# Sums of a seven-product layer moved to DVE and spread over earlier steps, norm spreads a step later, first residual reread from the input

## The chip, the cores and the metric

One core of a Trainium2 chip runs the whole program. The metric is the device time of one execution in microseconds (us), as the median of several runs. Five engines work from queues of their own, each in order: TensorE (PE) does matmuls, with its weight loads shown apart as PEld; VectorE (DVE), ScalarE (ACT) and GpSimd (POOL) do elementwise work; SyncE (SP) issues the DMAs.

## The reference

Two layers of a diffusion backbone over 512 latent and 256 context tokens of width 1024. Each layer is: a half-step SwiGLU FFN of width 2816, a token mixer, and a second half-step FFN.

```python
x = x + 0.5 * mod[2] * swiglu(modulate(x, mod[0], mod[1]), ffn1_w1, ffn1_w3, ffn1_w2)
...                              # the mixer, with mod[3..5]
x = x + 0.5 * mod[8] * swiglu(modulate(x, mod[6], mod[7]), ffn2_w1, ffn2_w3, ffn2_w2)

def modulate(x, shift, scale):
    return rms_norm(x) * (1 + scale) + shift
def swiglu(h, w1, w3, w2):
    return (jax.nn.silu(h @ w1) * (h @ w3)) @ w2
```

The context rows go through the same weights; in the second layer they stop after the mixer's keys. The nine vectors `mod` (adaLN) come from a 1024 x 9216 map of the conditioning.

## The kernel before, in words

Activations lie transposed: 128 features on the partitions, tokens along the row. `X` holds the residual in four tiles, `xn` the normalized input in eight tiles of 128 features, each as a high and a low half (`fp32r`), so that a product is three matmuls (`mm3`, L343 to L345): high by high, high by low, low by high. The tokens are worked in chunks: CL is all 512 latent ones, CLA and CLB their halves, CC the 256 of the context.

**Weights.** The class `Weights` reads the stream of weights in order. A unit is six blocks of 128 x 128, a set piece is four. `_make` splits one into halves: ACT copies the high half (L234), POOL subtracts (L235); for a set DVE adds some pieces first (L252 to L257). `ahead` is called at fixed places of the product loops and makes the next piece if it is within `ahead_by` units of the one in use. All tiles of 6 KB a row (`xn`, `X`, weights, `xs`, `xq`, hidden pairs, adaLN blocks) share 28 slots.

**The seven-product layers.** Three of the four FFNs (l=0 which=1 and 2, l=1 which=1) go through `ffn`. The first four hidden blocks (ff 0 to 3) are computed plainly: `up2_gen` makes ff 0 and 1 together, 16 steps for a chunk; `up_gen` makes one ff in four steps for a chunk, w1 first, then w3. Each ends in `tail`: ACT's silu into `gst` (L909), and a product with the second bank on DVE (L910). In the first FFN, which has two chunks, ff 0, 1 and the latent part of 2 come first, then ff 0, 1 of the context, then the list `rest`: (2, CC), (3, CL), (3, CC). In the other two, with three chunks, `rest` begins with (2, CL). The other 18 blocks are made pairwise by `seven_gen`: each pair and each of w1, w3 is a 2 x 2 block product in seven products instead of eight (tiles `sv`). Four of the seven read sums of the input blocks, which `Sums` prepares.

**Sums.** For each pair of feature tiles (i, i + 4) one job over two token blocks (the latent part) and one over the third (the context part): two additions of high and low halves into `xq` on POOL (L779), four operations that combine them on DVE (L782 to L785), two copies of the high half into `xs` on ACT (L788) and two differences on DVE (L789). Eight jobs, in two steps each, all placed between the steps of `rest`.

**Between the steps.** `cond` loads the conditioning and keeps its silu in PSUM for DVE; `more` does quarters of the adaLN map on DVE (L421) in the steps of `rest` after the first product, then after each of the seven products, at an even pace set by `calls`; `keep` stores a hidden pair and `save_x` the residual; `late` (the function `lambdas`) is a short chain of DVE and ACT operations with an exponential, once, in the first FFN.

**Norms.** `norm_gen` gives the next product its input in steps: `root` (column sums by PE, DVE, a power on POOL), `diag` (DVE builds `dg`, L529), `spread` (two or four matmuls of `dg` against ones, L543, which PE can do only when `dg` is there), and then DVE and ACT for the eight tiles. `Prep.tick(seg, step)` decides how many of these steps are issued after which step of the products around them.

**Order.** The scheduling is manual: each engine gets its instructions in the order in which the program traces them, and waits on semaphores.

Of the kernel before, what the change touches and what calls it, by code (L numbers as in the profile page):

```python
# [11 lines left out]
F32 = mybir.dt.float32  # L12
F32R = mybir.dt.float32r
AF = mybir.ActivationFunctionType
ALU = mybir.AluOpType
# [4 lines left out]
P = 128  # L20
D = 1024
NK = D // P
DFF = 2816
NF = DFF // P
LAT = 512
CTX = 256
TOK = LAT + CTX
# [14 lines left out]
CL = (0, LAT, 0)  # L42
# [8 lines left out]
PAIRS = [[8, 9], [10, 0, 1], [2, 3, 4], [5, 6, 7]]  # L51
# [5 lines left out]
SH = TOK // 2  # L57
# [240 lines left out]
def trunk(ctx: ExitStack, tc, a, out):  # L298
    nc = tc.nc
# [8 lines left out]
    drp = ctx.enter_context(tc.tile_pool(name="drp", bufs=1, space=DRAM))  # L308
    ctx.enter_context(tc.manual_schedule())

    def t6(shape, dt, name):
        return big.tile(shape, dt, name=name, tag="T6")
# [13 lines left out]
    def f(ap):  # L326
        return ap.bitcast(F32)
# [138 lines left out]
    W = Weights(nc, big, rawp, tmpp, a["wst"], a["wss"])  # L466


    X = [None] * 4
# [104 lines left out]
    def drain(g):  # L574
        for _ in g:
            pass

    class Prep:
# [15 lines left out]
        def tick(self, seg, step):  # L594
            for c, g in enumerate(self.gens):
                n = 0
                if len(self.chs) > 2:
                    n = step in (2, 5, 7) if seg == c + 1 else seg == c + 2
                elif c == 0:
                    n = (0, 1, 0, 1, 0, 1, 1, 1)[step] if seg == 1 else 2  # L600
                elif seg == 2:
                    n = (0, 0, 1, 0, 1, 0, 1, 1, 2, 2, 2, 2)[step]
                for _ in range(n):
                    next(g, None)

# [18 lines left out]
    def up2_gen(l, which, ffs, ch, xn, tail):  # L624
        c0, n, v = ch
        ps = [banks("up") for _ in ffs]
        touch(AF.Silu)
        for k in range(NK):
            for i, ff in enumerate(ffs):
                for w in range(2):  # L630
                    mm3(
                        ps[i][:, w, 0:n],
                        W.get((("w1", "w3")[w], l, which, k, ff)),
                        pair(xn[k], slice(c0, c0 + n)),
                        k == 0,
                        k == NK - 1,
                    )
                if i == 0:
                    yield
            W.ahead()  # L640
            yield
        for i, ff in enumerate(ffs):
            tail(ps[i][:, 0, 0:n], ps[i][:, 1, 0:n], n, ff, c0)
        yield

    def up_gen(l, which, ff, ch, xn, tail, single=False):
        c0, n, v = ch
        if single:
            ps = [bank(name="up1") for _ in range(2)]
        elif n > 256:  # L650
            ps = [p[:, w] for p in [banks("up")] for w in range(2)]
        else:
            ps = [p[:, w] for p in [bank((P, 2, 256), "upc")] for w in range(2)]
        for w in range(2):
            for k in range(NK):
                mm3(
                    ps[w][:, 0:n],
                    W.get((("w1", "w3")[w], l, which, k, ff)),
                    pair(xn[k], slice(c0, c0 + n)),
                    k == 0,  # L660
                    k == NK - 1,
                )
                if k % 4 == 3:
                    W.ahead()
                    if w and k == NK - 1:
                        tail(ps[0][:, 0:n], ps[1][:, 0:n], n, ff, c0)
                    yield
# [90 lines left out]
    def halves(ap):  # L758

        return ap.rearrange("p (b h q) -> p h b q", h=2, q=P)  # L760

    class Sums:
# [2 lines left out]
        def __init__(self, xn):  # L765
            self.xn, self.t = xn, [None] * 4

        def steps(self, b0, b1):

            c = slice(b0 * P, b1 * P)  # L770
            n = (b1 - b0) * P
            for i in range(4):
                if self.t[i] is None:
                    self.t[i] = [t6([P, 2, 2, SH], F32R, "xs") for _ in range(2)]
                x4 = t6([P, 4, n], F32, "xq")
                for e, x in enumerate((self.xn[i], self.xn[i + 4])):
                    hi, lo = [halves(f(x[:, z]))[:, :, b0:b1] for z in range(2)]
                    o = x4[:, 2 * e : 2 * e + 2].rearrange("p h (b q) -> p h b q", q=P)
                    nc.gpsimd.tensor_tensor(o, hi, lo, ALU.add)  # L779
                yield  # L780
                b11, b12, b21, b22 = [x4[:, z] for z in range(4)]
                nc.vector.tensor_tensor(b11, b11, b12, ALU.subtract)  # L782
                nc.vector.tensor_tensor(b12, b22, b12, ALU.subtract)
                nc.vector.scalar_tensor_tensor(b22, b11, -1.0, b22, ALU.mult, ALU.subtract)
                nc.vector.tensor_tensor(b21, b22, b21, ALU.add)  # L785
                for e, t in enumerate(self.t[i]):
                    v = x4[:, 2 * e : 2 * e + 2]
                    nc.scalar.activation(t[:, :, 0, c], v, AF.Copy)  # L788
                    nc.vector.tensor_tensor(t[:, :, 1, c], v, f(t[:, :, 0, c]), ALU.subtract)  # L789
                yield  # L790

        def moving(self, name, i):
# [85 lines left out]
    def ffn(l, which, whole, prep, after, late=None):  # L878
# [4 lines left out]
        stop = ADA_DONE[l, which]  # L883
        npl = SEVEN[l, which]
        gsave = drp.tile([NF // 2, P, 2, TOK], F32, name=f"gsave{l}{which}")
        xsave = drp.tile([4, P, 2, TOK], F32, name=f"xkeep{l}{which}")
        stage = {}


        first, todo = ada.count(0, ada.at) + ada.q, ada.count(ada.at, stop) - ada.q  # L890
        calls = (8 if late else 12) + 14 * (NF // 2 - npl - 2) + 2 * 2 * NK * (len(PAIRS) - 1)
        called = [0]

        def more(weight=1):
# [6 lines left out]
        def hidden(pair):  # L901
            stage[pair] = t6([P, 2, TOK], F32, "gst")

        def keep(pair):
            nc.sync.dma_start(out=gsave[pair], in_=stage.pop(pair))
# [5 lines left out]

        def save_x():
            for d2 in range(4):
                nc.sync.dma_start(out=xsave[d2], in_=X[d2])

        sums = Sums(xn)
        hidden(0)
        cond = ada.condition()
        if len(chs) == 2:
            for c, ch in enumerate(chs):  # L920
                seg = 2 + c
                for step, _ in enumerate(up2_gen(l, which, [0, 1], ch, xn, tail)):
                    if step < 2 * NK:
                        prep.half_tick(seg, step)
                if c == 0:
                    W.ahead_by = 1
                    hidden(1)
                    for step, _ in enumerate(up_gen(l, which, 2, ch, xn, tail, True)):
                        prep.tick(seg, NK + step)
            keep(0)  # L930
            prep.finish(1)
            save_x()
            late()
            rest = [(2, CC), (3, CL), (3, CC)]
        else:
            for c, ch in enumerate(chs):
                seg = 3 + c
                if c == 0:
                    for step, _ in enumerate(up2_gen(l, which, [0, 1], ch, xn, tail)):
                        if step < 2 * NK:  # L940
                            prep.half_tick(seg, step)
                else:
                    prep.finish(c)
                    if c == 1:
                        save_x()
                    for i, ff in enumerate((0, 1)):
                        for step, _ in enumerate(up_gen(l, which, ff, ch, xn, tail)):
                            prep.tick(seg, 4 * i + step)
            keep(0)
            hidden(1)  # L950
            rest = [(2, CL), (2, CC), (3, CL), (3, CC)]
# [1 line left out]
        for d2 in range(4):  # L953
            X[d2] = None
        W.ahead_by = 3
        parts = [sums.steps(0, 2), sums.steps(2, 3)]
        next(cond)
        for i, (ff, ch) in enumerate(rest):
            for step, _ in enumerate(up_gen(l, which, ff, ch, xn, tail, True)):
                if i == 0 and step == 1:  # L960
                    drain(cond)
                for _ in range(2 if len(rest) < 4 else 1):
                    while parts and next(parts[0], parts) is parts:
                        parts.pop(0)
                if i:
                    more()
        keep(1)
        for g in parts:
            drain(g)
        W.ahead_by, W.room = 5, 4  # L970


# [18 lines left out]

        def load_x(d2):
            X[d2] = t6([P, 2, TOK], F32, "x")
            nc.sync.dma_start(out=X[d2], in_=xsave[d2])

        def staged(pair):
            if pair not in stage:
# [21 lines left out]
        sums.t = None  # L1019
        W.ahead_by, W.room = 4, 3  # L1020
        load_x(0)
        ada.need(l, 3 * sub + 2)
        for gi, pairs in enumerate(PAIRS):
# [11 lines left out]
            for d in range(NK):  # L1035
                if gi == 0 and d % 2 == 0 and d < 6:
                    load_x(d // 2 + 1)
                for ch in whole:
                    c0, n, v = ch
# [1012 lines left out]
```

## Time and profile before

| | us |
|---|---|
| median of 3 runs | 2773.2 (2772.45 to 2774.08) |
| the profiled execution | 2769.08 |
| its span | 2767.3 |
| PE busy (share of the span) | 2651.7 (96%) |
| DVE busy | 1729.1 (62%) |
| POOL busy | 1267.9 (46%) |
| ACT busy | 996.6 (36%) |

An engine's busy time is the sum of its instructions' times without overlap. A wait is the idle time of an engine ahead of an instruction, put down to the instruction of another engine that ended last among those that it waits for. PE's granted clock was 0.980 of full speed on average.

### The profile page before, as it was taken

To read this page: it belongs to the slowest core of one execution; us is meant where nothing else is said; L and a number is where in the kernel's file an instruction comes from. 1 tells how busy PE (TensorE), PEld (TensorE's weight loads), DVE (VectorE), ACT (ScalarE), POOL (GpSimd) and SP (SyncE) were. 2 spreads that over 40 slices of the span, in tenths; PEclk is the share of its full clock that TensorE was granted. 3 is DMA by queue.
4 is the path that set the end of the run, shared out by engine and by line. 5 is a ranking of instruction groups with operands and counts; after the bars stand their busy time and mean duration, and the time that the engine had idled before them with its cause. 6 is when DMAs were issued, how large, how long until landed. Compare 5 with 4: busy or idle time off the path is not lost. (4 is left out here: it accounts for less than half of the span.)

```text
span 2767.3 us, 42854 instructions
## 1 busy us (share of the span) xinstructions
PE 2651.7 (96%) x16403; PEld 2449.0 (88%) x16403; DVE 1729.1 (62%) x3309; ACT 996.6 (36%) x1897; POOL 1267.9 (46%) x836
## 2 busy tenths in 40 slices
PE   8699999999999998999999989999999998899998
PEld 6699998999877887999989989998899887888887
DVE  4688866565778768777645677766465679621113
ACT  3333342233444443333322333342234444432222
POOL 2466685413212325667852366676433222444442
PEclk9899999999999998999999999999999999999999
DMA  6354456333213133443741334438415223233331
GB/s 239 119 174 157 149 197 232 117 104 118 80 53 139 58 111 96 145 138 110 276 151 42 126 107 129 148 100 317 162 62 175 90 79 115 87 93 103 104 101 37
DMA packets 130221, 355.47 MB, mean 128 GB/s; under 512 B 15456, under 2 KB 21472, under 8 KB 130016
## 3 DMA queue, kind: packets, MB, share of 16 engines
q1 hardware_dynamic: 130016, 352.73, 37.9%
q8 instruction: 129, 2.11, 0.3%
q14 instruction: 76, 0.62, 0.1%
HBM read 304.44 MB, written 44.04 MB: 126 GB/s over the span
## 5 line engine op out<-in xcount | busy, mean ns | idle before, releaser
L235 POOL TENSOR_TENSOR w<-wraw,w 128x768 fp32r<-128x768 f32 x288 | 537.2, 1884 | 815.3 <-ACT w L234 768.9
L343 PE MATMUL dn<-g,w 128*128 128x256 f32 (+1 forms) x1408 | 455.5, 323 | 0.0
L344 PE MATMUL dn<-g,w 128*128 128x256 f32 (+1 forms) x1408 | 455.3, 323 | 0.0
L235 POOL TENSOR_TENSOR ws<-wraw,ws 128x512 fp32r<-128x512 f32 x270 | 359.8, 1342 | 206.6 <-ACT ws L234 152.5
L345 PE MATMUL dn<-g,w 128*128 128x256 f32 (+1 forms) x1408 | 454.4, 323 | 0.0
L671 DVE SCALAR_TENSOR_TENSOR x<-dn,gt,x 128x256 f32<-128x256 f32 (+1 forms) x272 | 161.2, 593 | 294.6 <-PE dn L345 292.4
L421 DVE CUSTOM_DVE_ANT_0 araw<-araw,cB 128x512 f32<-128x512 f32 x448 | 302.0, 679 | 2.4
L343 PE MATMUL sv<-xs,ws 128*128 128x384 f32 x864 | 291.6, 338 | 8.2 <-ACT xs L788 8.2
L344 PE MATMUL sv<-xs,ws 128*128 128x384 f32 x864 | 291.6, 337 | 1.3 <-DVE xs L789 1.3
L345 PE MATMUL sv<-xs,ws 128*128 128x384 f32 x864 | 290.8, 337 | 0.0
L343 PEld LDWEIGHTS dn<-g,w 128*128 128x128 f32 x1408 | 268.0, 190 | 21.6
L345 PEld LDWEIGHTS dn<-g,w 128*128 128x128 f32 x1408 | 267.7, 190 | 21.2
L344 PEld LDWEIGHTS dn<-g,w 128*128 128x128 f32 x1408 | 268.0, 190 | 20.7
L234 ACT ACTIVATE w<-wraw 128x768 fp32r<-128x768 f32 x288 | 234.7, 835 | 114.4 <-DVE part L421 29.9
L343 PE MATMUL up<-xn,w 128*128 128x512 f32 (+1 forms) x656 | 235.3, 359 | 9.9 <-ACT gst L909 8.9
L343 PE MATMUL sv<-xn,ws 128*128 128x384 f32 x648 | 219.3, 338 | 26.4 <-ACT gst L909 25.6
L344 PE MATMUL up<-xn,w 128*128 128x512 f32 (+1 forms) x656 | 234.5, 358 | 2.6 <-DVE xn L559 2.4
L345 PE MATMUL up<-xn,w 128*128 128x512 f32 (+1 forms) x656 | 233.6, 356 | 0.0
L344 PE MATMUL sv<-xn,ws 128*128 128x384 f32 x648 | 218.5, 337 | 0.0
L345 PE MATMUL sv<-xn,ws 128*128 128x384 f32 x648 | 218.4, 337 | 0.0
L235 POOL TENSOR_TENSOR ws<-wsum,ws 128x512 fp32r<-128x512 f32 x108 | 148.7, 1377 | 93.5 <-ACT ws L234 71.6
L343 PEld LDWEIGHTS sv<-xs,ws 128*128 128x128 f32 x864 | 164.0, 190 | 11.2 <-ACT xs L788 10.9
(272 smaller groups left out, 6039.9 us busy)
## 6 DMA issues: line engine op xcount, KB each, us to landing
wraw<-in_wst_dram SPq DMA_DIRECT2D x288, 384.0 KB, 3.5
araw<-in_wadaT_dram SPq DMA_DIRECT2D x128, 512.0 KB, 4.7
wraw<-in_wss_dram SPq DMA_DIRECT2D x216, 256.0 KB, 2.8
gsave<-gst SPq DMA_DIRECT2D x24, 768.0 KB, 4.1
graw<-gsave SPq DMA_DIRECT2D x24, 768.0 KB, 6.9
xkeep<-x SPq DMA_DIRECT2D x12, 768.0 KB, 6.7
x<-xkeep SPq DMA_DIRECT2D x12, 768.0 KB, 8.8
ada<-in_wada_dram SPq DMA_DIRECT2D x16, 512.0 KB, 10.1
```

Of the source, the lines that this page charges most:

```text
L234: self.nc.scalar.activation(hi, raw, AF.Copy)
L235: self.nc.gpsimd.tensor_tensor(lo, raw, hi.bitcast(F32), ALU.subtract)
L343: nc.tensor.matmul(o, s[0], m[0], start=first, stop=False, skip_group_check=shared)
L344: nc.tensor.matmul(o, s[0], m[1], start=False, stop=False, skip_group_check=shared)
L345: nc.tensor.matmul(o, s[1], m[0], start=False, stop=last, skip_group_check=shared)
L421: nc.vector.tensor_tensor_reduce(out=raw[:, 2], in0=raw[:, h], in1=self.c[v][:, h], op0=ALU.mult, op1=ALU.add, scale=1.0, scalar=0.0, accu ...
L671: nc.vector.scalar_tensor_tensor(x, ps, gt[l][:, sub, d, ch[2] : ch[2] + 1], x, ALU.mult, ALU.add)
```

## The change

- `Sums`: the two additions of a job go from POOL to DVE. A job has four parts now (additions; the four operations; the copies; the differences), and `steps()` chains the eight jobs into one sequence in which a job's differences and the next job's additions are issued together: 25 steps.
- Where the steps stand: in the first FFN one after each of the 16 steps of the context's `up2_gen`, the others in `rest`; in the other two FFNs one after each of the four steps of (1, CC), the last product before `rest`, the others in `rest`: two after each step of a latent product, one after each of a context product.
- `ahead_by` is 2 during (1, CC) in the FFNs with three chunks. `cond` finishes after the fourth step of `rest`, not the second. `more` is called in `rest` only where `late` is given, and `calls` counts accordingly.
- `Prep.tick`: with three chunks the third step of a norm (`spread`) is issued together with the fourth, after the first step of the next segment. With two chunks it is issued one step later, and for the second chunk `root` and `diag` one step earlier.
- In the first FFN the residual is not stored; `load_x` reads it again from the input `xT`. In the others it is stored as before.

```diff
@@ -595,11 +595,11 @@
             for c, g in enumerate(self.gens):
                 n = 0
                 if len(self.chs) > 2:
-                    n = step in (2, 5, 7) if seg == c + 1 else seg == c + 2
+                    n = step in (2, 5) if seg == c + 1 else (2 if step == 0 else 1) if seg == c + 2 else 0
                 elif c == 0:
-                    n = (0, 1, 0, 1, 0, 1, 1, 1)[step] if seg == 1 else 2
+                    n = (0, 1, 0, 1, 0, 0, 1, 2)[step] if seg == 1 else 2
                 elif seg == 2:
-                    n = (0, 0, 1, 0, 1, 0, 1, 1, 2, 2, 2, 2)[step]
+                    n = (0, 1, 0, 1, 0, 0, 0, 1, 2, 2, 2, 3)[step]
                 for _ in range(n):
                     next(g, None)
 
@@ -765,28 +765,43 @@
         def __init__(self, xn):
             self.xn, self.t = xn, [None] * 4
 
-        def steps(self, b0, b1):
-
+        def job(self, i, b0, b1):
+
+            tt = nc.vector.tensor_tensor
             c = slice(b0 * P, b1 * P)
-            n = (b1 - b0) * P
-            for i in range(4):
-                if self.t[i] is None:
-                    self.t[i] = [t6([P, 2, 2, SH], F32R, "xs") for _ in range(2)]
-                x4 = t6([P, 4, n], F32, "xq")
-                for e, x in enumerate((self.xn[i], self.xn[i + 4])):
-                    hi, lo = [halves(f(x[:, z]))[:, :, b0:b1] for z in range(2)]
-                    o = x4[:, 2 * e : 2 * e + 2].rearrange("p h (b q) -> p h b q", q=P)
-                    nc.gpsimd.tensor_tensor(o, hi, lo, ALU.add)
-                yield
-                b11, b12, b21, b22 = [x4[:, z] for z in range(4)]
-                nc.vector.tensor_tensor(b11, b11, b12, ALU.subtract)
-                nc.vector.tensor_tensor(b12, b22, b12, ALU.subtract)
-                nc.vector.scalar_tensor_tensor(b22, b11, -1.0, b22, ALU.mult, ALU.subtract)
-                nc.vector.tensor_tensor(b21, b22, b21, ALU.add)
-                for e, t in enumerate(self.t[i]):
-                    v = x4[:, 2 * e : 2 * e + 2]
-                    nc.scalar.activation(t[:, :, 0, c], v, AF.Copy)
-                    nc.vector.tensor_tensor(t[:, :, 1, c], v, f(t[:, :, 0, c]), ALU.subtract)
+            if self.t[i] is None:
+                self.t[i] = [t6([P, 2, 2, SH], F32R, "xs") for _ in range(2)]
+            x4 = t6([P, 4, (b1 - b0) * P], F32, "xq")
+            for e, x in enumerate((self.xn[i], self.xn[i + 4])):
+                hi, lo = [halves(f(x[:, z]))[:, :, b0:b1] for z in range(2)]
+                tt(x4[:, 2 * e : 2 * e + 2].rearrange("p h (b q) -> p h b q", q=P), hi, lo, ALU.add)
+            yield
+            b11, b12, b21, b22 = [x4[:, z] for z in range(4)]
+            tt(b11, b11, b12, ALU.subtract)
+            tt(b12, b22, b12, ALU.subtract)
+            nc.vector.scalar_tensor_tensor(b22, b11, -1.0, b22, ALU.mult, ALU.subtract)
+            tt(b21, b22, b21, ALU.add)
+            yield
+            parts = [(x4[:, 2 * e : 2 * e + 2], t[:, :, 0, c], t[:, :, 1, c]) for e, t in enumerate(self.t[i])]
+            for v, hi, lo in parts:
+                nc.scalar.activation(hi, v, AF.Copy)
+            yield
+            for v, hi, lo in parts:
+                tt(lo, v, f(hi), ALU.subtract)
+
+        def steps(self):
+
+            todo = [self.job(i, b0, b1) for b0, b1 in ((0, 2), (2, 3)) for i in range(4)]
+            for n, g in enumerate(todo):
+                if n == 0:
+                    next(g)
+                    yield
+                for _ in range(2):
+                    next(g)
+                    yield
+                next(g, None)
+                if n + 1 < len(todo):
+                    next(todo[n + 1])
                 yield
 
         def moving(self, name, i):
@@ -883,12 +898,15 @@
         stop = ADA_DONE[l, which]
         npl = SEVEN[l, which]
         gsave = drp.tile([NF // 2, P, 2, TOK], F32, name=f"gsave{l}{which}")
-        xsave = drp.tile([4, P, 2, TOK], F32, name=f"xkeep{l}{which}")
+        if late:
+            xkept = [a["xT"][:, 2 * d2 : 2 * d2 + 2] for d2 in range(4)]
+        else:
+            xkept = drp.tile([4, P, 2, TOK], F32, name=f"xkeep{l}{which}")
         stage = {}
 
 
         first, todo = ada.count(0, ada.at) + ada.q, ada.count(ada.at, stop) - ada.q
-        calls = (8 if late else 12) + 14 * (NF // 2 - npl - 2) + 2 * 2 * NK * (len(PAIRS) - 1)
+        calls = (8 if late else 0) + 14 * (NF // 2 - npl - 2) + 2 * 2 * NK * (len(PAIRS) - 1)
         called = [0]
 
         def more(weight=1):
@@ -911,17 +929,20 @@
 
         def save_x():
             for d2 in range(4):
-                nc.sync.dma_start(out=xsave[d2], in_=X[d2])
+                nc.sync.dma_start(out=xkept[d2], in_=X[d2])
 
         sums = Sums(xn)
         hidden(0)
         cond = ada.condition()
+        added = sums.steps()
         if len(chs) == 2:
             for c, ch in enumerate(chs):
                 seg = 2 + c
                 for step, _ in enumerate(up2_gen(l, which, [0, 1], ch, xn, tail)):
                     if step < 2 * NK:
                         prep.half_tick(seg, step)
+                    if c and step < 2 * NK:
+                        next(added, None)
                 if c == 0:
                     W.ahead_by = 1
                     hidden(1)
@@ -929,7 +950,6 @@
                         prep.tick(seg, NK + step)
             keep(0)
             prep.finish(1)
-            save_x()
             late()
             rest = [(2, CC), (3, CL), (3, CC)]
         else:
@@ -946,6 +966,10 @@
                     for i, ff in enumerate((0, 1)):
                         for step, _ in enumerate(up_gen(l, which, ff, ch, xn, tail)):
                             prep.tick(seg, 4 * i + step)
+                            if c == 2 and i:
+                                next(added)
+                        if c == 2 and i == 0:
+                            W.ahead_by = 2
             keep(0)
             hidden(1)
             rest = [(2, CL), (2, CC), (3, CL), (3, CC)]
@@ -953,20 +977,17 @@
         for d2 in range(4):
             X[d2] = None
         W.ahead_by = 3
-        parts = [sums.steps(0, 2), sums.steps(2, 3)]
         next(cond)
         for i, (ff, ch) in enumerate(rest):
             for step, _ in enumerate(up_gen(l, which, ff, ch, xn, tail, True)):
-                if i == 0 and step == 1:
+                if i == 0 and step == 3:
                     drain(cond)
-                for _ in range(2 if len(rest) < 4 else 1):
-                    while parts and next(parts[0], parts) is parts:
-                        parts.pop(0)
-                if i:
+                for _ in range(2 if ch is CL else 1):
+                    next(added, None)
+                if i and late:
                     more()
         keep(1)
-        for g in parts:
-            drain(g)
+        drain(added)
         W.ahead_by, W.room = 5, 4
 
 
@@ -991,7 +1012,7 @@
 
         def load_x(d2):
             X[d2] = t6([P, 2, TOK], F32, "x")
-            nc.sync.dma_start(out=X[d2], in_=xsave[d2])
+            nc.sync.dma_start(out=X[d2], in_=xkept[d2])
 
         def staged(pair):
             if pair not in stage:
```

## Rows read from the trace of the kernel before

**Rows 1.** Waits of PE, whole span: waiting line, releaser; us in total, times, longest.
```profile
PE sv L343 <- ACT gst L909: 25.6, 3, 13.4
PE bc L543 <- DVE dg L529: 16.7, 6, 5.5
...
PE sv L343 <- ACT xs L788: 8.2, 5, 2.2
...
PE sv L344 <- DVE xs L789: 1.3, 2, 0.8
```

**Rows 2.** Timeline of PE, 82 to 135: start, duration, instruction, [wait, releaser].
```profile
82.99 0.28 PE L343 MATMUL up<-xn,w 128*128 128x256 f32 x1
...
88.75 0.40 PE L343 MATMUL up<-xn,w 128*128 128x512 f32 x1
...
99.43 0.39 PE L345 MATMUL up<-xn,w 128*128 128x512 f32 x1
108.73 0.58 PE L343 MATMUL up<-xn,w 128*128 128x256 f32 x1 [8.91 <-ACT gst L909]
...
130.41 0.69 PE L343 MATMUL sv<-xn,ws 128*128 128x384 f32 x1 [13.43 <-ACT gst L909]
...
134.38 0.34 PE L343 MATMUL sv<-xs,ws 128*128 128x384 f32 x1
```

**Rows 3.** Timeline of PE at the first seven products of the two later layers.
```profile
1063.02 0.69 PE L343 MATMUL sv<-xn,ws 128*128 128x384 f32 x1 [6.47 <-ACT gst L909]
...
1080.36 0.34 PE L343 MATMUL sv<-xn,ws 128*128 128x384 f32 x1
...
1082.44 0.33 PE L343 MATMUL sv<-xs,ws 128*128 128x384 f32 x1
...
1603.11 0.69 PE L343 MATMUL sv<-xn,ws 128*128 128x384 f32 x1 [5.65 <-ACT gst L909]
...
1619.66 0.34 PE L343 MATMUL sv<-xn,ws 128*128 128x384 f32 x1
```

**Rows 4.** Instructions on tile xq, POOL: count, ns least/median/most, first and last start.
```profile
L779 POOL TENSOR_TENSOR xq<-xn x48: 721/1234/1489, 89.0 to 1608.2; 128x512 f32<-128x512 f32 x24, 128x256 f32<-128x256 f32 x24
```

**Rows 5.** Timeline of DVE, 75 to 119.
```profile
75.54 0.49 DVE L559 SCALAR_TENSOR_TENSOR xn<-val,modT,xn 128x256 fp32r<-128x256 f32 x1 [0.18 <-ACT xn L564]
...
83.94 0.22 DVE L1901 TENSOR_TENSOR lpr<-lv 128x64 f32<-128x64 f32 x1
...
97.88 1.50 DVE L782 TENSOR_TENSOR xq<-xq 128x256 f32<-128x256 f32 x1 [3.21 <-POOL xq L779]
...
105.80 0.41 DVE L782 TENSOR_TENSOR xq<-xq 128x256 f32<-128x256 f32 x1
...
109.04 0.41 DVE L910 TENSOR_TENSOR gst<-gst,up 128x256 f32<-128x256 f32 x1
...
115.51 0.29 DVE L783 TENSOR_TENSOR xq<-xq 128x128 f32<-128x128 f32 x1
...
118.67 0.69 DVE L253 TENSOR_TENSOR wsum<-wsum,wraw 128x512 f32<-128x512 f32 x1
119.28 0.68 DVE L254 TENSOR_TENSOR wraw<-wraw 128x512 f32<-128x512 f32 x1
```

**Rows 6.** Timeline of DVE, 2395 to 2398.
```profile
2395.72 2.25 DVE L529 TENSOR_TENSOR dg<-ident,two 128x512 fp32r<-128x512 f32 x1
```

**Rows 7.** Timeline of ACT and of POOL, 86 to 89.
```profile
86.26 0.83 ACT L234 ACTIVATE w<-wraw 128x768 fp32r<-128x768 f32 x1
...
87.17 1.85 POOL L235 TENSOR_TENSOR w<-wraw,w 128x768 fp32r<-128x768 f32 x1 [15.81 <-ACT w L234]
```

**Rows 8.** DMA issues (page, part 6): count, KB each, us from issue to landing.
```profile
araw<-in_wadaT_dram SPq DMA_DIRECT2D x128, 512.0 KB, 4.7
```

**Rows 9.** Timeline of PE at two norm spreads.
```profile
998.45 0.80 PE L543 MATMUL bc<-dg,onesr 128*128 128x256 f32 x2 [5.49 <-DVE dg L529]
...
2398.03 0.80 PE L543 MATMUL bc<-dg,onesr 128*128 128x256 f32 x2 [4.57 <-DVE dg L529]
```

## The prediction

> **What bounds the kernel now.** I read the engine table first: TensorE (PE) is busy nearly all of the span, no other engine comes near it, so only time that PE loses counts. The waits of PE over the whole span come next [rows 1]. The reader is to see four groups that this change can touch: one on `gst` (25.6 us in three waits), two on `xs` (8.2 and 1.3) and one on `dg` (16.7 in six). The timeline of PE around the first hidden layer [rows 2] places the largest: PE is ready for the last plain product (3, CC) at 99.7, starts it at 108.73 after 8.91 us, and starts the seven-product part at 130.41 after 13.43 us more. The same starts of the other two layers stand in [rows 3]. After each wait PE also runs at the lower of its two clock levels: the 12 matmuls from 130.41 take 3.97 us [rows 2], where 12 of that shape take 2.08 later (1080.36 to 1082.44) [rows 3]. `gst` is only the last link: its activation stands in ACT's queue behind copies `xs`, which wait for DVE's sums, which wait for POOL's additions `xq` (48 of 1.23 us) [rows 4].
>
> **First layer (l=0, which=1).** Waits lost now: 8.91 + 13.43 = 22.34. Slow clock: from 108.73 to 130.41 are 21.68 us, less 13.43 of wait is 8.25 for 48 matmuls that took 5.76 at full clock (82.99 to 88.75) [rows 2], so 2.5; and 3.97 - 2.08 = 1.9. Together 26.7.
>
> After the change the additions are DVE's, and 16 of the 25 steps stand in DVE's and ACT's queues ahead of the tails of the context up2 product. DVE is free for them once the context norm is done, at 75.54 + 0.49 = 76.0 [rows 5]. A latent job is four operations and two differences, which took 3.24 us from 105.80 to 109.04 with POOL idle [rows 5], and two additions of 512 columns. No row shows such an addition on DVE with these strided operands. Below it lies nothing under the 0.61 between starts of the plain 512-column addition (0.69 long) [rows 5]; above it the dearest DVE operation beside a busy POOL, 2.25 [rows 6]; I take 0.65, as the plain one is the nearest row and POOL's additions, which made 256-column operations 1.50 instead of 0.41 [rows 5], are gone. A job is then 3.24 + 1.3 = 4.54, four are 18.2, so 94.2. The first context job (0.29 for each operation [rows 5], about 0.33 between starts, two half-length additions) has its four operations done at 96.2.
>
> What is queued behind it: ACT holds the copies of that job, then both `gst` tails, the exponentials of `lambdas`, and only then the copy of weight unit 9, the second one that ff 3 needs. DVE still does the two differences, the next additions and the two tail products, some 2.4 us, so `lambdas` begins at 98.6. From its first DVE operation to the copy of unit 9 were 83.94 to 86.26, 2.3 us [rows 5, 7]; the copy and POOL's subtraction end 2.76 later (86.26 to 87.17 + 1.85) [rows 7]. Unit 9 is ready at 103.7. PE wants it after the 18 matmuls of unit 8: (3, CL) starts at 88.75 and its matmuls are (99.43 - 88.75)/47 = 0.227 apart [rows 2], so at 92.8, and it can do two matmuls (0.45) on the copied half alone. New wait: 103.7 - 92.8 - 0.45 = 10.4 us, and I charge the 2.5 of slow clock that followed the 8.91 wait. Behind this the rest is in time: PE ends (3, CC) near 119, and all sums, reckoned on in the same way, near 116. Gain: 26.7 - 10.4 - 2.5 = 13.8. SP's store of the first hidden pair now waits for those tail products, until about 98.6 instead of 84, and behind it stand the loads of `condition` and of the first weight set; they land near 105, which is when ACT and DVE come to them, so nothing. POOL loses its additions and keeps only subtractions. If DVE is slower than assumed, 1 us more for a job costs 4 here.
>
> **Second and third hidden layers (l=0 which=2; l=1 which=1).** Waits: of the 25.6 on `gst` the other two, 12.2, and all of `xs`, 9.5 [rows 1]: 21.7. Slow clock: from the first seven-product matmul to the start of the fourth product are 17.34 us (1063.02 to 1080.36) and 16.55 (1603.11 to 1619.66); less the 9.5 of `xs` waits and less 6 x 2.08 for six products that is 11.9 [rows 3]. Together 33.6.
>
> Here four steps move ahead of the last context product and eight fall under each latent one. From the first of them to the second product of the seven, where the sums are first read, PE has 4.3 + 10.9 + 5.8 + 10.9 + 5.8 + 2.1 = 39.8 us of matmuls (spacings of [rows 2, 3]). DVE has four jobs of 4.54, four of 2.9 (additions 0.7, operations 1.3, differences 0.9), tails of about 2.2 and three weight additions of 0.69 [rows 5]: 34.1. It keeps up with 5.7 us to spare, so I take both waits as gone. `condition` at step 3 puts ACT's wait for its DMA behind the first jobs; I cost that at nothing, since ACT has little else there. What is late next: `more` no longer runs in this stretch, so the first adaLN block is fetched only after the first of the seven products, and DVE waits for it with the sums' tails behind it. A load takes 4.7 us [rows 8]; PE needs the first of those tails at the fifth product, 4 x 2.08 = 8.3 us on. I charge 0.5 for each layer, between 0 and 4.7. Gain 32.6. The moved quarters (some eight a layer, one DVE operation each) spread over about 200 us.
>
> **Norms.** The spread matmuls wait for `dg` on DVE [rows 9]. With three chunks they move behind the first 12 matmuls of the next chunk, 12 x 0.12 = 1.44 us, and DVE's order stays: the 5.49 wait gives back 1.4, not more, as `dg` is no earlier. With two chunks the roots go a step ahead as well, and the spread moves a step later: at 2398.03 PE waited 4.57 because `dg` was slow (2.25 [rows 6]) and late; the order ahead puts it before POOL's row of weight subtractions: 4.0 gained, and 2.0 of clock, near the 2.5 above. The other four `dg` waits are 16.7 - 5.5 - 4.6 = 6.6 [rows 1, 9]; each of three can give at most 1.44, and the one at the very end is not moved: 2.5 of at most 4.3. Sum 9.9.
>
> **First residual from the input.** Four stores go from SP's queue, and X frees its slots before the sums take theirs. PE waits for neither now: nothing, bounds 0 and 1 us.
>
> **Sum.** 13.8 + 32.6 + 9.9 = 56.3 us. The profiled execution took 2769.1; less 56.3 is 2712.8. The median of the runs is 4.1 above that execution: 2716.9.
>
> **Rivals.**
> A, the forecast: 2717, chance 0.52.
> B, unit 9 does not come late, because DVE's jobs are shorter or ACT's order differs: 12.9 more, 2704; with the 5.5 and the other waits wholly gone 2697. For it: before, the unit was ready 3.8 us early. Against: its copy stands after `lambdas` in program order. 0.16.
> C, POOL's weight subtractions slow the additions to 1.50 each [rows 5]. First layer: ten additions lie ahead of unit 9, 8.5 us more, gain 5.3. The other two: 16 additions each, 13.6 less 5.7 spare is 7.9 of wait, and the 11.9 of clock stays: 33.6 - 15.8 - 11.9 - 1 = 4.9, or some 10 if the clock recovers in part. With the norms 20 to 25 us: 2748 to 2753. For it: 1.50 against 0.41 in one kind of operation. Against: the slow ones ran beside POOL's additions, and only single subtractions are left here. 0.20.
> E, slower: the same mechanism at full price. An addition of c us costs 42 x (c - 0.65) over the three layers (10 + 16 + 16), and at worst the clock's 11.9 stays too; the gain of 56.3 - 11.9 + 11.4 (both spare times) = 55.8 is used up at c = 1.98. An addition that first waits out a whole subtraction of 1.85 [rows 7] is 2.54, which costs 79: 24 slower, 2797. 0.07. Between C and E lies the stretch within 0.2% of before, 0.05.
>
> The Trainium skill, "SBUF — State Buffer", section "Who interferes with whom", speaks for E: a DVE instruction with both inputs in SBUF and a GpSimd one that reads SBUF share a port, and the later one is blocked for the other's whole length. By that rule each of the 48 additions is exposed. The trace agrees that it happens (1.50 against 0.41) and shows that an unaccompanied one is not slowed; by it alone the time would be E's 2797 only if nearly every addition met a subtraction, and I keep E at its 0.07.
>
> **Numbers.** About 0.2% (5.5 us) can be told from no change. Faster: A, B, C = 0.88; same 0.05; slower 0.07. The range takes in B's far end and C's near end, 2697 to 2748, with about 2 in 10 left out; A's own is 2709 (a shorter stay of unit 9 by 8) to 2726 (both adaLN loads at 4.7).
>
> **What would show it.** Right: in the first layer no PE wait on `gst` over 2 us, and one new wait of about 10 us on weight `w` (ACT's copy, then POOL) inside (3, CL), seven-product part starting near 119; `xq` additions on DVE at 0.6 to 0.7; in the other two layers no `gst` or `xs` wait at the start, at most 2 us on `sv` from late tails; `dg` waits of about 4, 1.4, and under 1 where 4.57 was. Wrong: additions over 1.2 us, a start of the first seven-product part before 110 (B), or a DVE that idles for an adaLN block while PE waits.

## The result, and the profile after

The changed kernel takes 2734.1 us (median; 2729.1 to 2739.8), 0.986 of before [0.9838, 0.9881]: 39.1 us faster where 56.3 were forecast. The profiled execution took 2736.7 with a span of 2734.9; the two spans differ by 32.4, and the other 6.7 is which executions were profiled: before's lay 4.1 under its median, this one 2.6 over. The sums below are in spans. A line number is that of the kernel shown: the copy into `gst` is L909 before and L927 after, the differences of `Sums` L789 before and L790 after.

PE's waits over the whole span, after (waiting line, releaser; us in total, times, longest; to be read against [rows 1]):

```profile
PE sv L343 <- DVE u L851: 9.7, 2, 5.6
PE bc L543 <- DVE dg L529: 8.5, 3, 4.3
PE up L343 <- ACT w L234: 7.6, 1, 7.6
...
PE upc L344 <- DVE xn L559: 4.7, 5, 1.6
...
PE up L343 <- ACT xn L564: 2.7, 3, 1.8
...
PE nat L343 <- DVE val L563: 2.2, 2, 1.1
...
PE sv L343 <- ACT gst L927: 1.5, 1, 1.5
...
PE up L344 <- DVE xn L559: 1.1, 4, 0.3
```

Of 25.6 us on `gst` 1.5 is left, the waits on `xs` are gone, `dg` has halved. New are the waits on weight `w`, which was forecast, and on `u`, which was not. Those on the norm's own outputs `xn` and `val` grew from 3.4 (2.4 and 1.0 on `xn`) to 10.7.

**First layer.** PE's timeline after (start, duration, instruction, [wait, releaser]; against [rows 2]):

```profile
84.52 0.28 PE L343 MATMUL up<-xn,w 128*128 128x256 f32 x1
...
102.18 0.80 PE L343 MATMUL up<-xn,w 128*128 128x512 f32 x1 [7.63 <-ACT w L234]
...
104.07 0.79 PE L345 MATMUL up<-xn,w 128*128 128x512 f32 x1 [0.67 <-POOL w L235]
...
120.43 0.44 PE L343 MATMUL sv<-xn,ws 128*128 128x384 f32 x1 [1.49 <-ACT gst L927]
...
122.62 0.33 PE L343 MATMUL sv<-xs,ws 128*128 128x384 f32 x1
```

From the start of (2, CC) to the thirteenth matmul of the seven products, with the same work between: 82.99 to 134.38 before [rows 2], 84.52 to 122.62 now. That is 51.4 against 38.1, a gain of 13.3. The new wait stands where the prediction put it, on unit 9 inside (3, CL), 7.63 + 0.67 long instead of 10.4. Of the 38.1 these two and the 1.49 before the seven products are waits, and some 3.6 more are the slow clock (0.56 granted from 102.2 to 110.5). ACT's timeline shows the queue that makes the new wait: `gst`, a table load, the exponentials (`dots`), and only then the copies of `w`:

```profile
97.23 0.64 ACT L927 ACTIVATE gst<-up 128x256 f32<-128x256 f32 x2
97.89 1.28 ACT L1926 ACT_TABLE_LOAD   x1
...
101.19 0.20 ACT L1926 ACTIVATE dots<-dots 128x2 f32<-128x2 f32 x1 [1.06 <-DVE dots L1925]
101.30 1.56 ACT L234 ACTIVATE w<-wraw 128x768 fp32r<-128x768 f32 x2
```

**Later layers.** PE's timeline after (against [rows 3]):

```profile
1045.78 0.34 PE L343 MATMUL sv<-xn,ws 128*128 128x384 f32 x1
...
1059.91 0.69 PE L343 MATMUL sv<-xs,ws 128*128 128x384 f32 x1 [5.64 <-DVE u L851]
...
1066.58 0.33 PE L343 MATMUL sv<-xn,ws 128*128 128x384 f32 x1
...
1573.24 0.34 PE L343 MATMUL sv<-xn,ws 128*128 128x384 f32 x1
...
1585.84 0.69 PE L343 MATMUL sv<-xs,ws 128*128 128x384 f32 x1 [4.10 <-DVE u L851]
...
1592.38 0.33 PE L343 MATMUL sv<-xn,ws 128*128 128x384 f32 x1
```

Both seven-product parts start without a wait, as forecast. At the fifth product PE stops for `u`, a sum of partial products that DVE should have made. Six products at 2.08 us [rows 3] are 12.48; from the first to the seventh passed 20.80 (1045.78 to 1066.58) and 19.14 (1573.24 to 1592.38 in the third layer), so 8.3 and 6.7 are lost here to the wait and to the slow clock after it (0.50 granted from 1059.9 to 1064.9). DVE's and SP's timelines say why:

```profile
1048.59 0.42 DVE L928 TENSOR_TENSOR gst<-gst,up 128x256 f32<-128x256 f32 x1
1057.48 0.69 DVE L421 CUSTOM_DVE_ANT_0 araw<-araw,cB 128x512 f32<-128x512 f32 x1 [8.48 <-DMA araw<-in_wadaT_dram]
...
1059.30 0.55 DVE L851 TENSOR_TENSOR u<-sv,p 128x384 f32<-128x384 f32 x1
```

```profile
1049.03 0.33 SPq L923 DMA_DIRECT2D gsave<-gst  x1
...
1050.84 1.01 SPq L411 DMA_DIRECT2D araw<-in_wadaT_dram  x2
```

DVE's next instruction is a quarter of an adaLN block that is still on its way, and `u` stands behind it. The block was asked for at 1050.84 only: its issue stands in SP's queue behind the store of the second hidden pair, which waits for DVE's last `gst` (1048.59), and behind two loads of weights. SP issued nothing between 1021.7 and that store. The block landed 6.6 us after its issue (1057.48 - 1050.84), in the third layer 5.1.

**Norms.** PE's timeline after (against [rows 9], and a stretch of the second two-chunk norm):

```profile
988.24 0.79 PE L543 MATMUL bc<-dg,onesr 128*128 128x256 f32 x2 [4.33 <-DVE dg L529]
...
2360.97 0.40 PE L543 MATMUL bc<-dg,onesr 128*128 128x256 f32 x2
...
2370.97 0.39 PE L344 MATMUL upc<-xn,w 128*128 128x256 f32 x1 [1.39 <-DVE xn L559]
```

The 5.49 fell by 1.2 and the 4.57 went, both as forecast. But the spread comes later and the matmuls on its result do not, so PE now waits for `xn` itself: 1.39 here, and 4.7 in all five waits of `upc`. Waits on the norms' steps (`dg`, `xn`, `val`) add up to 8.5 + 4.7 + 2.7 + 2.2 + 1.1 = 19.2; with the steps as before they are 20.6 (e2 below).

### The profile page after: what moved, and what is told of

Its sections match the earlier page's. It is cut to its first block, busy times and chain, and to the rows that moved or that the text cites. A ratio compares the mean times of both kernels' runs of the same rounds, so it can differ in the third digit from the quotient of the medians.

```text
span 2734.9 us, 42815 instructions
## 1 busy us (share of the span) xinstructions
PE 2645.8 (97%) x16403; PEld 2445.7 (89%) x16403; DVE 1733.9 (63%) x3357; ACT 996.2 (36%) x1897; POOL 1215.6 (44%) x788
## 4 chain that ended last, share of the span: by engine, by line
PE 53%; DVE 9%; issue 3%; ACT 2%; POOL 1%; DMA 0%; SPq 0%; POOLq 0%; ACTq 0%; DVEq 0%
PE sv L343 6%; PE sv L345 6%; PE sv L344 6%; PE dn L343 6%; PE dn L344 6%; PE dn L345 6%; PE up L344 3%; PE up L343 3%; PE up L345 3%; DVE xn L559 1%; DVE acc L496 1%; PE upc L344 1%; DVE xq L777 1%; PE upc L345 1%; PE upc L343 1%
## 5 line engine op out<-in xcount | busy, mean ns | idle before, releaser
L343 PE MATMUL up<-xn,w 128*128 128x512 f32 (+1 forms) x656 | 236.2, 360 | 10.4 <-ACT w L234 7.6
L343 PEld LDWEIGHTS sv<-xs,ws 128*128 128x128 f32 x864 | 163.8, 190 | 10.4 <-DVE u L851 10.4
```

What stands on the lines that cost most here:

```text
L343: nc.tensor.matmul(o, s[0], m[0], start=first, stop=False, skip_group_check=shared)
```

## The experiments

All are timed against the kernel before on the same chip (2771.3, 2771.5 and 2772.3 us in the three sessions) and read beside the changed kernel's 2734.1. Ratios are to before.

**e1_prefetch: the adaLN block asked for earlier.** In the list `rest`, in the later layers only:

```diff
                 if i and late:
                     more()
+                if not late and i == 2 and step == 0:
+                    ada.fetch(min(ada.at + 1, stop - 1))
```

> The changed kernel, with the first two adaLN blocks of the two later seven-product layers fetched at the start of (3, CL) instead of after the first of the seven products. Theory (the load): DVE's 8.5 us of idleness for that block is what held PE 5.6 and 4.1 us and then at the lower clock, 8.3 + 6.7 = 15 us in all, so the wait of PE on u is gone and the time is 2719 (ratio 0.980). Rival (too much DVE work there anyway): u stays late behind quarters and weight additions, the wait halves at most, 2730 or more (0.985).

2719.2 us (2717.4 to 2722.4), 0.9812 [0.9798, 0.9825]. PE runs through the fifth product, and SP sends the blocks ahead of the store:

```profile
1050.56 0.33 PE L343 MATMUL sv<-xs,ws 128*128 128x384 f32 x1
```

```profile
1021.51 0.80 SPq L411 DMA_DIRECT2D araw<-in_wadaT_dram  x2
...
1045.48 0.33 SPq L923 DMA_DIRECT2D gsave<-gst  x1
```

The 15 us read from the trace (8.3 + 6.7) came back whole. The late load is shown as the cause.

**e2_ticks_old: the norms' steps as before**, all else as changed:

```diff
-                    n = (0, 1, 0, 1, 0, 0, 0, 1, 2, 2, 2, 3)[step]
+                    n = (0, 0, 1, 0, 1, 0, 1, 1, 2, 2, 2, 2)[step]
```

(and likewise the rule for three chunks and that for the first of two).

> The changed kernel with the norm steps (tick) of the kernel before. Theory (read from the two traces): the later spreads give 1.2 and 1.4 us in the three-chunk layers and 0.6 twice, and nothing with two chunks, since 4.6 of waiting for dg became 4.7 of waiting for xn: 2734 + 4 = 2738 (0.987). Rival (the prediction's term): 9.9 us are lost, 2744 (0.9895).

2734.3 us, 0.9861 [0.9846, 0.9876]: no difference. The rival's 9.9 us (0.9895) lie outside the interval; the theory's 4 (0.987) lie inside it, so that the time alone does not exclude them, but PE's waits speak against them. `dg` waits as long as before [rows 1], and `xn` less than after:

```profile
PE bc L543 <- DVE dg L529: 16.7, 6, 5.5
PE up L344 <- DVE xn L559: 2.4, 6, 1.0
...
PE up L343 <- ACT xn L564: 1.5, 3, 0.6
```

20.6 us here against 19.2: PE waits the same time for another of the norm's instructions.

**e4_adds_pool and e5_dve_only: the engine apart from the place.** e4 is the changed kernel with its additions on POOL, e5 the kernel before with its additions on DVE:

```diff
-    tt(x4[...], hi, lo, ALU.add)                       # e4
+    nc.gpsimd.tensor_tensor(x4[...], hi, lo, ALU.add)
-    nc.gpsimd.tensor_tensor(o, hi, lo, ALU.add)        # e5
+    nc.vector.tensor_tensor(o, hi, lo, ALU.add)
```

> The changed kernel with the two additions of each job back on POOL; the steps stay where the change put them. Theory (the place of the steps is the larger part): a job takes some 6 us instead of 4.6, so in the first layer unit 9 comes 5 to 6 us later, the other two layers still end their sums in time: 2742 (0.989). Rival (the engine is the larger part): the waits on gst and xs come back at the start of the seven products, 2757 or more (0.994).

> The kernel before with only the additions moved from POOL to DVE; steps, norms, residual and adaLN quarters as before. If the engine alone is the larger part: DVE has some 34 us of work in 22 us of plain products in the first layer and 40 in 33 in the others, so about 12 of 22 and 6 of 11 us of wait remain, 2745 (0.990). If the place of the steps is the larger part: the chain is no shorter, since each addition only changes its queue, 2765 or more (0.997).

e4: 2734.0 us, 0.9862 [0.9849, 0.9876], the same as with DVE. e5: 2761.5 us, 0.9962 [0.995, 0.9975], some 10 of the 39. In e5 PE's waits keep their places:

```profile
PE sv L343 <- ACT gst L909: 19.5, 3, 12.8
...
PE sv L343 <- ACT xs L788: 10.0, 4, 2.9
PE up L343 <- ACT gst L909: 7.1, 1, 7.1
```

So the engine is worth something only while the sums are late. In the changed kernel's places it is worth nothing. POOL then runs its additions ahead of DVE: in e4 it starts them at 71.0, and DVE does the first operation on them at 77.1, where in the changed kernel DVE starts its own additions at 77.5. In all of e4 DVE stands 1.3 us for POOL's additions, before the change 18.0. e4 came out better than either theory allowed. No run moves the steps alone: `cond`, `more` and `ahead_by` moved with them, and what each of these is worth was not told apart. The `xq` additions of e4 (count; ns least/median/most; first and last start):

```profile
L777 POOL TENSOR_TENSOR xq<-xn x48: 735/1230/1531, 71.0 to 1564.9; 128x512 f32<-128x512 f32 x24, 128x256 f32<-128x256 f32 x24
```

**e7_store_x and e10_store_early: the first residual.** e7 is the changed kernel with the first residual stored and reloaded as before; e10 issues the same four stores at the start of the layer:

```diff
             keep(0)
             prep.finish(1)
+            save_x()                      # e7
...
         if len(chs) == 2:
+            save_x()                      # e10, in its place
```

> The changed kernel (2734.1) with the residual stored and reloaded from the store in the first layer too, as before. Theory: nothing on PE's path, 2734 (0.986), within 1 us. Rival: the four stores hold SP for 4 us ahead of condition and the set weights, or keep four slots from the sums, and the first seven-product part starts 3 us or more later: 2737 (0.987).

> The kernel of e7_store_x with one edit: in the first hidden layer the four stores of the residual are issued at its start, ahead of the store of the first hidden pair, where the queue of SP has nothing to send (after 61 us it issues nothing until 98), instead of behind that store. If what the stored residual cost (e7: 2741.5 against 2734.1) is its place in SP's queue, in front of the loads of condition and of the weight sums, which then land about 4 us later while ACT waits for them (6.26 us on cb in e7), the time goes back to that of the changed kernel, 2734 to 2735, and ACT's wait for cb at the copies is gone. If it is the transfers themselves, the reload or the slots that the residual holds, it stays near 2741.

e7: 2741.5 us (2740.2 to 2743.4), 0.9892 [0.9879, 0.9906], 7.4 slower than the changed kernel in medians (the intervals just touch; those of e7 and e10 do not). SP, ACT and PE in e7:

```profile
98.20 0.33 SPq L920 DMA_DIRECT2D gsave<-gst  x1
98.58 3.96 SPq L929 DMA_DIRECT2D xkeep<-x  x4
102.65 5.07 SPq L400 DMA_DIRECT2D cb<-in_cB_dram  x4
...
111.79 0.60 ACT L404 ACTIVATE cB<-cb 128x512 f32<-128x512 f32 x1 [6.26 <-DMA cb<-in_cB_dram]
...
125.31 0.69 PE L343 MATMUL sv<-xn,ws 128*128 128x384 f32 x1 [7.63 <-ACT gst L924]
```

The stores stand behind the first hidden pair's store, which the change moved from 84 to 99 (98.20 here), and the condition's loads stand behind them. ACT waits for these with the last copies of the sums queued behind, and PE's wait before the seven products is 7.63 where it was 1.49. e10: 2731.0 us (2730.6 to 2733.4), 0.9854 [0.9839, 0.9869]:

```profile
38.17 3.66 SPq L929 DMA_DIRECT2D xkeep<-x  x4
...
117.52 0.44 PE L343 MATMUL sv<-xn,ws 128*128 128x384 f32 x1 [0.35 <-ACT gst L924]
```

The same bytes, sent at 38 instead of 98, cost nothing. The price was their place in the queue; that the issue time (3.96) and the transfers share in it was not told apart.

**e6_units_early, e8_spread_6, e9_all: can the first layer and the norms give more?** All on e1. e6 lets weight units be made further ahead; e8 moves one step of a two-chunk norm; e9 has both, and issues the `lambdas` after the sums:

```diff
                 if c == 0:
-                    W.ahead_by = 1
+                    W.ahead_by = 3                                     # e6
-                    n = (0, 1, 0, 1, 0, 0, 0, 1, 2, 2, 2, 3)[step]
+                    n = (0, 1, 0, 1, 0, 0, 1, 1, 2, 2, 2, 2)[step]     # e8
-            late()
+            if late and step == 20: late()       # e9, in the first seven-product part
```

> The kernel of e1_prefetch (2719.2), with ahead_by 3 instead of 1 while the latent part of ff 2 runs in the first layer, so that weight units 9 and 10 are copied and subtracted near 72, before the sums' steps enter ACT's queue. Theory (the copy queues behind the sums' copies): the waits on w (7.6 and 0.8) and 2.4 us of slow clock go; PE then comes early to the bank of (2, CC), whose silu still stands behind the sums, and to the second product, so some 5 us come back as waits on gst or xs: 2714 (0.979). Rival (the sums themselves are the bound of this stretch): all comes back, 2719 (0.981).

> The kernel of e1_prefetch (2719.2), with the spread of the second of two chunks after half step 6 as before, but its root and diag at 1 and 3 as changed. Theory (the later spread only turned the dg wait into waits of the next product on xn): DVE's first operations of the norm get ahead of the tail of up2, the waits on xn (4.7 us and the clock after them) go, at most 1 us of dg wait comes: 2713 (0.979). Rival (DVE beside POOL's weight subtractions is the bound either way): the same waits under another name, 2719 (0.981).

> The kernel of e1_prefetch with the edits of e6_units_early and e8_spread_6, and lambdas issued after step 20 of the first seven-product part instead of ahead of the rest list. Theory: lambdas held 2.5 us of DVE's and two table loads of ACT's time in the stretch that bounds the first layer; sum of the two others plus 3 to 4 us: 2705 (0.975). Rival (these are one bound, not three): no better than the better of e6 and e8, 2713.

2721.3, 2719.9 and 2722.8 us (0.9821, 0.9812, 0.9826): none beats e1's 2719.2, and e9 lies some 10 us above even its rival. In e6 the wait on `w` is gone and two on the sums stand in its place; in e9 these are one:

```profile
103.25 0.39 PE L343 MATMUL up<-xn,w 128*128 128x256 f32 x1 [3.67 <-ACT gst L927]
...
116.04 0.69 PE L343 MATMUL sv<-xn,ws 128*128 128x384 f32 x1 [5.29 <-ACT gst L927]
```

```profile
116.26 0.69 PE L343 MATMUL sv<-xn,ws 128*128 128x384 f32 x1 [10.55 <-ACT gst L927]
```

The start at 116 did not move although the exponentials and their table load (1.28 on ACT in the changed kernel) had left the queues before it. Nor was the sums' own work the bound there, since DVE stood idle in it. In e9, DVE and ACT:

```profile
107.20 1.62 DVE L790 TENSOR_TENSOR xs<-xq,xs 128x256 fp32r<-128x256 f32 x2 [5.23 <-ACT xs L787]
...
103.24 1.88 ACT L404 ACTIVATE cB<-cb 128x512 f32<-128x512 f32 x3 [3.63 <-DMA cb<-in_cB_dram]
```

It is e7's mechanism again: the condition's loads, behind the store.

**e11_cond_early: e9 with these loads ahead of the store.**

```diff
+            next(cond)
             keep(0)
             prep.finish(1)
...
         W.ahead_by = 3
-        next(cond)
+        if not late:
+            next(cond)
```

> The kernel of e9_all with one edit: the four loads of condition are issued by SP ahead of the store of the first hidden pair, not behind it. In e9_all the four operations of DVE's last jobs were done at 102.0, and then DVE stood 5.23 us for ACT's copies, ACT 3.63 us for the first of the condition's loads, which SP had issued only at 98.15, behind the store; the first seven-product part began 10.55 us late. If the place of these loads in SP's queue is what bounds the first layer there, the 10.55 falls by some 5 us and the time from 2722.8 to about 2717. If the loads then wait for other things (their slots, or the weight sums' loads, which stay behind the store), or DVE's sums bound it on their own, the wait keeps over 9 us and the time is 2721 to 2723.

2716.0 us (2713.9 to 2717.3), 0.9796 [0.9779, 0.9812]; 6.8 under e9.

```profile
70.04 4.24 SPq L400 DMA_DIRECT2D cb<-in_cB_dram  x4
...
104.12 1.65 DVE L790 TENSOR_TENSOR xs<-xq,xs 128x256 fp32r<-128x256 f32 x2 [0.80 <-ACT xs L787]
...
113.20 0.69 PE L343 MATMUL sv<-xn,ws 128*128 128x384 f32 x1 [6.15 <-ACT gst L927]
```

DVE's 5.23 is 0.80, PE's wait is 4.4 shorter, and PE starts 3.1 earlier; where the rest of the 6.8 came from is open. What is left of the wait, 6.15, ends a stretch in which DVE has no gap over 0.8 us, so that its own work is probably the limit by now; no run tested this. This is the quickest version that ran, 18 us under the changed kernel; against e1 it is 3.2 in medians with overlapping intervals, from different sessions.

## Why the prediction was right, and where its terms failed

The time lies in the stated range, 2697 to 2748, and the two large terms name the waits that went. But 2734.1 is above what A, the forecast, gave itself (2709 to 2726). The range held it only because it reached to C's near end, and C did not come about: that is luck. The prediction's own signs were mixed. The first layer's came out as written, but PE waited 5.6 and 4.1 on `sv` where at most 2 was allowed, and a DVE that idles for an adaLN block while PE waits was named as a sign of being wrong.

- **First layer, forecast 13.8: right**, measured 13.3, with the forecast wait in the forecast place (8.3 for 10.4). So unit 9 did come late, and rival B fell. The sum came out closer than its parts: the wait was 2.1 shorter than forecast, while the slow clock took 3.6 for 2.5 and the 1.5 on `gst` had no term.
- **Later layers, forecast 32.6: the waits went, and 18.5 was gained.** From PE being ready for the seven products to the seventh passed 30.1 and 28.4 before (ready at 1063.02 - 6.47 and 1603.11 - 5.65, the fourth product at 1080.36 and 1619.66 [rows 3], and three more of 2.08) and 20.8 and 19.1 after. The term that failed is the adaLN load, "I charge 0.5 for each layer, between 0 and 4.7": it cost 8.3 and 6.7. The prediction saw the late fetch and what stands behind it, but counted a load from its issue at the median 4.7 [rows 8]. It left out that the issue itself waits in SP's queue behind a store that waits for DVE, that the load took 6.6 and 5.1 behind other transfers, and that the wait brings the slow clock with it. e1 shows the size: without it the span is 46.7 shorter than before (2767.3 to 2720.6) where 56.3 were forecast, and the 9.6 still missing is the next term.
- **Norms, forecast 9.9: nothing that shows** (e2). Each forecast `dg` wait went as said; what was not asked is what is late next. The spread's result is read at once, so a later spread turns into a wait for `xn`. In e8 `upc` waits 2.9 for `xn` where it waited 4.7 in e1, PE waits 0.5 for `dg` instead, and the time is the same (2719.9 against 2719.2).
- **Residual, "nothing, bounds 0 and 1 us": 7.4 in the place where it was** (e7), nothing in another (e10). The prediction knew that the hidden pair's store moves from 84 to 98 and carries the queue behind it; it did not put the four stores into that queue. This gain lies inside the 13.3 of the first layer, which the forecast had reached with the stores already gone.
- **Additions on DVE (rivals C and E).** Of the 48, 42 took no more than 0.69: 0.68 to 0.69 with 512 columns, where 0.65 was taken, and 0.41 to 0.42 with 256. The other six took 1.51 to 2.34, each beside a subtraction of POOL, and all in the later layers, where PE did not wait for the sums. So what C and E describe does happen, but six times only. C's argument against it, that the slow operations ran beside POOL's additions, does not hold: these six met single subtractions, as the 2.25 of [rows 6] had. Count, ns least/median/most, first and last start:

```profile
L777 DVE TENSOR_TENSOR xq<-xn x48: 410/684/2336, 77.5 to 1571.9; 128x512 f32<-128x512 f32 x24, 128x256 f32<-128x256 f32 x24
```

- **The sum.** 13.3 + 18.5 leaves 0.6 of the 32.4 in spans for the norms and all else.

## What to carry to other kernels

When a step moves, write down each queue as it will stand, store by store: a store that waits for late work holds every load issued behind it, and an instruction that waits for such a load holds all behind it on its own engine. Price a load from when its issue can leave the queue, not from when the program asks for it. Before counting a wait as gained, look at the next reader of the same result: moving the wait is not removing it.

## What the runs showed of the hardware

DVE's operations on the sums lengthened beside POOL's subtractions where the subtraction had begun first, but few of them met one. In the first layer after the change the same 128-column operation took 0.29 at 96.25 and 1.95 at 102.21, when POOL had just begun to subtract for unit 9 (two subtractions one after the other, the first ending at 104.01):

```profile
102.20 3.64 POOL L235 TENSOR_TENSOR w<-wraw,w 128x768 fp32r<-128x768 f32 x2 [29.31 <-ACT w L234]
...
102.21 1.95 DVE L782 SCALAR_TENSOR_TENSOR xq<-xq 128x128 f32<-128x128 f32 x1
```

The six slow additions show the same. Each began 0.06 to 0.43 after a subtraction and ended 0.28 to 0.55 after its end. Four additions that began 0.17 to 0.28 ahead of a subtraction were not lengthened; two of these subtractions took 2.22, where the median of their kind is 1.85, and two did not lengthen (1.29).

The Trainium skill, "SBUF — State Buffer", section "Who interferes with whom", says that a DVE instruction with two inputs in SBUF contends with a GpSimd one that reads SBUF, over ports that only one of them can hold, and that the order of issue decides which is blocked. The six and the 1.95 agree.

The Trainium skill, "DMA: Bandwidth & Descriptors", section "Issuing engines are not separate DMA queues", calls the time to initiate a DMA usually small beside the DMA itself. For one store this agrees: four held SP for 3.96 us (e7), about 1 each, and such a store took 6.7 to land (median in e7). But the issues add up in SP's queue, and the order there, with loads behind a waiting store, decided 7 us (e7 against the changed kernel, e11 against e9).
